# Gate and up of a SwiGLU feed-forward as 2x2 block products, seven in place of eight for three of eight k-tile pairs

## The chip, the core and the metric

One core of a Trainium2 chip runs the whole kernel. The metric is the device time of one execution in microseconds (us); smaller is better. The kernel before was timed three times: 2159.31, 2161.99 and 2163.21 us, with a median of 2161.99 us.

The engines are named as in the profile: PE is the matrix engine (PEld its weight loads, which run beside the products), DVE the vector engine, ACT the scalar engine, POOL the general one, SP the queue that issues the DMAs.

## What is computed

Two decoder layers over a sequence of 256 tokens of width 2048, float32. Layer 0 has a mixer with stick-breaking and differential attention heads, layer 1 a latent-attention mixer; each mixer, and each feed-forward, is followed by a layer norm of the residual sum. The change concerns the feed-forward, of which there is one in each layer:

```python
FFN_DIM = -(-8 * D_MODEL // (3 * 256)) * 256      # 5632

def swiglu_ffn(x, w_gate, w_up, w_down):
    return (jax.nn.silu(x @ w_gate) * (x @ w_up)) @ w_down

for layer in range(DEPTH):                        # 2
    ...
    x = layer_norm(DN_ALPHA * x + mix, ln_g[layer, 0], ln_b[layer, 0])
    x = layer_norm(DN_ALPHA * x + swiglu_ffn(x, ffn_w_gate[layer], ffn_w_up[layer], ffn_w_down[layer]),
                   ln_g[layer, 1], ln_b[layer, 1])
```

## The kernel before

**Precision.** Every large product is made of three. Each float32 operand is split into a rounded part hi (type fp32r) and the rest lo, and the product is hi·hi + hi·lo + lo·hi. `split` (L123) makes the parts: ACT copies the source into hi (L124), then DVE subtracts hi from the source and writes lo (L125). So each weight tile costs one ACT and one DVE instruction, and DVE's one waits for ACT's.

**Tiles.** The 256 tokens are two tiles t of 128 (NT = 2). The contraction over 2048 is 16 k-tiles of 128. The transposed x stands in SBUF for a whole feed-forward as hi and lo (`xTh`, `xTl`).

**A unit.** `ffn` (L448) walks through 11 chunks c of 512 hidden columns, in three parts of 4, 4 and 3 chunks. For one chunk (a unit) it calls `gemm` (L248) with gate and up side by side. For each of 16 k-tiles, `load` fetches 128x512 of gate and 128x512 of up into one 128x1024 tile w (two DMAs on SP, L273) and splits it. `products` (L278) then issues for each t six products of 128x128 by 128x512: hi·hi and hi·lo for gate, the same for up (L292, L293), then lo·hi for both (L295). A unit is 16 x 2 x 6 = 192 products into four PSUM banks. At its end `evac` (L461) does for each t a Silu of gate on ACT (L463) and a multiplication by up on DVE (L464). Two ticks later four PE transposes (L130) and a split (into `Rh`, `Rl`) turn the 128x512 result into the left side for the down product. After each part, two `gemm` calls (L494) multiply it by the weights of down and `add_to_x` (L402) adds into x; after the last one come the norm's statistics (L409) and the layer norm.

**What sets the order.** `tick` advances background work by one step after each k-tile. The source's order is only a priority: the program that puts the kernel together orders the instructions of each engine by when their inputs and buffers are there. `lag` (L275 on, used with `NORM_LAG` = 7 for the first unit of a feed-forward) lets t = 1 start seven k-tiles after t = 0, while the norm of the second tile ends; `advance` (L314, called at L328) says how far t = 1 may go.

**Buffers.** Weight tiles w have 5 buffers. The parts hi and lo have 6 buffers each; `halves` (L239) adds three more pairs out of buffers idle in this stage (`t6`, `gv`, `gk`) while `roomy` is set, which it is from the second half of the out projection to the end of the feed-forward: 9 pairs. In the mixers it is off: 6 pairs. PSUM has six banks "g" for products and two "m" for transposes and attention. The pool `ga` has two tiles of 128x2048, the norm's parameters among others; `stage` has four of 128x512.

Of the kernel before, what the change touches and what calls it, by code (L numbers as in the profile page):

```python
# [13 lines left out]
F32 = mybir.dt.float32  # L14
F32R = mybir.dt.float32r
I32 = mybir.dt.int32
AF = mybir.ActivationFunctionType
ALU = mybir.AluOpType
AX = mybir.AxisListType

P = 128
S = 256
NT = 2
D = 2048
KD = D // P
# [25 lines left out]
class Net:  # L51
# [11 lines left out]
    ATTENTION_DELAY = 3  # L63
    ACROSS = 3
    KEY_GROUP = 8
    HIDDEN_DELAY = 2
    BANKS = (6, 2)

# [170 lines left out]
    def halves(self, n):  # L239

        pools = [(self.hp, "h", self.lp, "l")] * self.BUFS[3]
        if self.roomy:
            pools += [(self.t6, "t6", self.gv, "v"), (self.gk, "kT", self.gv, "v"), (self.t6, "t6", self.t6, "t6")]
        hp, ht, lp, lt = pools[self.slot % len(pools)]
        self.slot += 1
        return hp.tile([P, n], F32R, tag=ht, name="h"), lp.tile([P, n], F32R, tag=lt, name="l")

    def gemm(self, src, kts, lhs, widths, evac=None, each=None, lag=0, apart=0, fine=0, across=0, before_end=None):  # L248
        nc = self.nc
        total = sum(widths)  # L250
        offs = [sum(widths[:c]) for c in range(len(widths))]
        ps, units = {}, {}

        def unit_width(k):
            return 512 if kts.index(k) < fine else 1024

        def load(k):
            units[k] = []
            aps = src(k)
            width = unit_width(k)  # L260
            for a0 in range(0, total, width):
                n = min(width, total - a0)
# [12 lines left out]
                self.split(hi, lo, w)  # L275
                units[k].append((hi, lo))

        def products(i, t, cs=None):  # L278
            k = kts[i]
            if i == 0:  # L280
                ps[t] = [self.psg.tile([P, 512], F32, tag="g", name="g") for _ in widths]
            first, last = i == 0, i == len(kts) - 1
            xh, xl = lhs(k, t)
            parts = []
            for c, n in enumerate(widths):
                width = unit_width(k)
# [12 lines left out]
            if last and evac:  # L299
                evac(t, ps[t])  # L300

        n = len(kts)
        tail = 2 if apart else 0
        second = 0

        def step(i, t):
            if i < n - max(tail, across):
                products(i, t)
            elif tail and i == n - 1:
                for c in range(len(widths)):  # L310
                    for k in range(n - tail, n):
                        products(k, t, slice(c, c + 1))

        def advance(end):  # L314
            nonlocal second
            while second < end:
                step(second, 1)
                second += 1

        for i in range(n):  # L320
            with ExitStack() as order:
                if fine:
                    for ins in self.first[:2 if i else 1]:
                        order.enter_context(self.tc.issue_after(ins.ins))
                load(kts[i])
            step(i, 0)
            self.tick()
            advance(min(i + 1 - lag, n - apart))  # L328
        if across:
            advance(n)  # L330
            for c in range(len(widths)):
                for t in range(NT):
                    for k in range(n - across, n):
                        products(k, t, slice(c, c + 1))
        advance(n - 1)
        if before_end:
            before_end()
        advance(n)
# [106 lines left out]
            self.norm_chunk(t)  # L445


    def ffn(self, layer, final):  # L448
        nc = self.nc
        wg, wu, wd = (self.io[n][layer] for n in ("ffn_w_gate", "ffn_w_up", "ffn_w_down"))  # L450
        parts = [range(0, 4), range(4, 8), range(8, 11)]
        for pi, part in enumerate(parts):
            self.new_res()
            for ci, c in enumerate(part):
                sl = slice(c * 512, (c + 1) * 512)

                def src(k):
                    rs = slice(k * P, (k + 1) * P)
                    return [((0, 512), wg[rs, sl]), ((512, 1024), wu[rs, sl])]

                def evac(t, ps, ci=ci):  # L461
                    sg = self.stage.tile([P, 512], F32, tag="st", name="sg")
                    nc.scalar.activation(sg, ps[0], AF.Silu)  # L463
                    nc.vector.tensor_tensor(sg, sg, ps[1], op=ALU.mult)  # L464

                    def transposed():
                        tp = self.bank()
                        self.transposes(tp, sg, 4)
                        ks = slice(4 * ci, 4 * ci + 4)
                        ts = slice(t * P, (t + 1) * P)  # L470
                        self.split(self.Rh[:, ks, ts], self.Rl[:, ks, ts], tp.rearrange("p (k n) -> p k n", k=4))

                    self.later(self.HIDDEN_DELAY, transposed)

                self.gemm(src, range(KD), self.from_x, [512, 512], evac, lag=self.NORM_LAG if c == 0 else 0)
                self.roomy = True
            n = 4 * len(part)
            last = pi == len(parts) - 1
            self.stats = {}
            k0 = part[0] * 4  # L480
            for half in range(2):
                if last and half == 1:
                    self.norm_params(layer, 1)

                def src(k, half=half, k0=k0):
                    return [((0, 1024), wd[(k0 + k) * P:(k0 + k + 1) * P, half * 1024:(half + 1) * 1024])]

                def each(t, c, ps, half=half, pi=pi, last=last):
                    self.add_to_x(t, half * 2 + c, ps, pi == 0, last)
                    if last and half == 1 and c == 1:  # L490
                        self.layer_norm(t, final)

                before_next = last and half == 1
                self.gemm(src, range(n), self.from_res, [512, 512], each=each,  # L494
                          apart=self.TILES_APART if before_next else 0,
                          before_end=(lambda: self.turn(0, 0)) if before_next and not final else None)
        self.roomy = False
# [204 lines left out]
    def mixer1(self):  # L702
# [40 lines left out]
        def rope_key():  # L743
            ps = self.bank()
            for t in range(NT):
                o = ps[:, t * P:(t + 1) * P]
                for k in range(KD):
# [139 lines left out]
```

## Time and profile before

| | |
|---|---|
| median of three runs | 2161.99 us |
| the profiled execution, its own time | 2163.7 us |
| its span, first to last instruction | 2162.0 us |
| PE busy | 2137.5 us, 99% of the span |
| PE weight loads busy | 1765.7 us, 82% |
| DVE busy | 1191.2 us, 55% |
| ACT busy | 936.9 us, 43% |
| DMA | 399.56 MB, mean 185 GB/s |
| mean granted PE clock | 0.997 of full speed |

The profile is of one execution. An engine is busy while it runs an instruction; a share of busy time is a mean over stages. Products on PE overlap in the record, so the time that one takes is read from the distance between the starts of two, not from its own duration. The idle time of an engine is put down to whatever released it. In the view by stretch a row gives the stretch (us from the start of the span) and its length, then the busy us, with instruction counts, of PE, PEld, DVE, ACT and POOL, then the granted PE clock, the DMA share and GB/s. In a timeline a row gives start, duration, engine, line, operation, out<-in and, in brackets, the idle time before it and what ended it; several alike in a row are merged (x2, x4).

### The profile page before, as it was taken

The page shows a single profiled execution, that of the slowest core. Times are in us where ns is not written, and L with a number is a line of the kernel's source. Part 1 is how long each engine was busy: PE and PEld are TensorE (multiplying, and loading weights), DVE is VectorE, ACT ScalarE, POOL GpSimd, SP SyncE. Part 2 cuts the span into 40 slices and gives each one's busy share as a digit, 9 for nine tenths or more (in the row PEclk, how much of TensorE's full clock was granted, in tenths as well). Part 3 has the DMA queues.
Part 4 walks back from the last instruction along what each step waited for, and adds up shares of the span by engine and source line. Part 5 has one row for each costly group of instructions (what it writes and reads, how often), then busy time and mean ns, then how long its engine had stood idle before and what let it go on. Part 6 is the DMA issues. An engine that isn't in the chain of part 4 may idle for free.

```text
span 2162.0 us, 25896 instructions
## 1 busy us (share of the span) xinstructions
PE 2137.5 (99%) x9734; PEld 1765.7 (82%) x9734; DVE 1191.2 (55%) x1340; ACT 936.9 (43%) x1111; POOL 51.9 (2%) x71
## 2 busy tenths in 40 slices
PE   8999999999999999999999999999999999999997
PEld 7888888888888888888887788888888888888886
DVE  7545566754554455444546665675544554445545
ACT  4554445354433444434424456444444344434441
POOL 0001010000000000000000100000000000000000
PEclk9999999999999999999999999999999999999999
DMA  7654647465556655566645443746556665556662
GB/s 261 196 164 147 194 142 249 146 221 188 193 187 195 190 189 187 193 197 190 222 151 156 160 138 103 257 142 224 186 191 193 192 192 185 191 193 192 191 228 77
DMA packets 171949, 399.56 MB, mean 185 GB/s; under 512 B 20400, under 2 KB 21040, under 8 KB 170800
## 3 DMA queue, kind: packets, MB, share of 16 engines
q1 hardware_dynamic: 171824, 397.91, 57.2%
q8 instruction: 76, 1.25, 0.2%
q14 instruction: 49, 0.40, 0.1%
HBM read 395.74 MB, written 2.10 MB: 184 GB/s over the span
## 4 chain that ended last, share of the span: by engine, by line
PE 93%; DVE 3%; issue 2%; ACT 1%; DMA 1%; POOL 0%; SPq 0%; DVEq 0%; POOLq 0%; ACTq 0%
PE g L293 29%; PE g L292 29%; PE g L295 29%; PE m L130 2%; DVE l L125 1%; PE m L560 0%; PE m L840 0%; PE m L841 0%; DVE x L438 0%; DMA x<-x 0%; DVE x L437 0%; DMA w<-sb_diff_w_out 0%; ACT sc L581 0%; ACT h L124 0%; DVE bs L409 0%
## 5 line engine op out<-in xcount | busy, mean ns | idle before, releaser
L125 DVE TENSOR_TENSOR l<-w,h 128x1024 fp32r<-128x1024 f32 (+1 forms) x737 | 892.2, 1219 | 836.9 <-ACT h L124 793.8
L124 ACT ACTIVATE h<-w 128x1024 fp32r<-128x1024 f32 (+1 forms) x737 | 769.5, 1053 | 1023.0 <-PE g L295 783.6
L292 PE MATMUL g<-h,xTh 128*128 128x512 f32 x1856 | 732.6, 396 | 1.0 <-ACT xTh L124 0.7
L293 PE MATMUL g<-l,xTh 128*128 128x512 f32 x1856 | 724.5, 392 | 0.5 <-DVE l L125 0.5
L295 PE MATMUL g<-h,xTl 128*128 128x512 f32 x1856 | 575.4, 391 | 0.0
L295 PEld LDWEIGHTS g<-h,xTl 128*128 128x128 f32 x1856 | 349.6, 188 | 73.8
L292 PEld LDWEIGHTS g<-h,xTh 128*128 128x128 f32 x1856 | 349.5, 189 | 73.3 <-ACT h L124 2.4
L293 PEld LDWEIGHTS g<-l,xTh 128*128 128x128 f32 x1856 | 349.8, 189 | 71.8 <-DVE l L125 1.8
L292 PE MATMUL g<-h,Rh 128*128 128x512 f32 x960 | 377.9, 394 | 0.0
L293 PE MATMUL g<-l,Rh 128*128 128x512 f32 x960 | 374.9, 390 | 0.0
L295 PE MATMUL g<-h,Rl 128*128 128x512 f32 x960 | 299.0, 390 | 0.0
L295 PEld LDWEIGHTS g<-h,Rl 128*128 128x128 f32 x960 | 180.3, 188 | 37.8
L292 PEld LDWEIGHTS g<-h,Rh 128*128 128x128 f32 x960 | 180.4, 188 | 36.7 <-DVE v L816 0.3
L293 PEld LDWEIGHTS g<-l,Rh 128*128 128x128 f32 x960 | 180.6, 188 | 36.2
L405 DVE SCALAR_TENSOR_TENSOR x<-x,g 128x512 f32<-128x512 f32 x64 | 40.9, 681 | 37.8 <-PE g L295 37.7
L124 ACT ACTIVATE Rh<-m 128x512 fp32r<-128x512 f32 x60 | 35.8, 596 | 58.3 <-PE m L130 41.5
L138 POOL TENSOR_TENSOR rr<-rv,mhalf 128x1 f32<-128x1 f32 (+1 forms) x16 | 13.0, 815 | 1703.2 <-DVE rv L136 1703.2
L125 DVE TENSOR_TENSOR Rl<-m,Rh 128x512 fp32r<-128x512 f32 x60 | 41.5, 691 | 20.1 <-ACT Rh L124 16.4
L463 ACT ACTIVATE sg<-g 128x512 f32<-128x512 f32 x44 | 26.2, 596 | 19.5 <-PE g L295 18.4
L464 DVE TENSOR_TENSOR sg<-sg,g 128x512 f32<-128x512 f32 x44 | 29.8, 684 | 7.6 <-ACT sg L463 7.6
L124 ACT ACTIVATE xTh<-m 128x512 fp32r<-128x512 f32 x30 | 17.7, 591 | 29.8 <-PE m L130 29.8
L130 PE MATMUL m<-ident,x 128*128 128x128 f32 x128 | 22.1, 288 | 8.2 <-DMA x<-x 6.0
(172 smaller groups left out, 853.5 us busy)
## 6 DMA issues: line engine op xcount, KB each, us to landing
w<-ffn_w_gate SPq DMA_DIRECT2D x352, 256.0 KB, 2.7
w<-ffn_w_up SPq DMA_DIRECT2D x352, 256.0 KB, 3.0
w<-ffn_w_down SPq DMA_DIRECT2D x176, 512.0 KB, 3.7
w<-sb_diff_w_in SPq DMA_DIRECT2D x95, 512.0 KB, 4.3
w<-sb_diff_w_out SPq DMA_DIRECT2D x32, 512.0 KB, 4.7
w<-mla_w_out SPq DMA_DIRECT2D x32, 512.0 KB, 4.3
w<-mla_w_in SPq DMA_DIRECT2D x16, 512.0 KB, 3.6
w<-mla_w_kv_up SPq DMA_DIRECT2D x16, 512.0 KB, 4.5
```

Of the source, the lines that this page charges most:

```text
L124: a = self.nc.vector.tensor_copy(hi, src) if whole else self.nc.scalar.activation(hi, src, AF.Copy)
L125: b = self.nc.vector.tensor_tensor(lo, src, hi.bitcast(F32), op=ALU.subtract)
L130: self.nc.tensor.transpose(ps[:, k * P:(k + 1) * P], src[:, k * P:(k + 1) * P], self.ident)
L138: nc.gpsimd.tensor_tensor(r, v, self.mhalf[:, 0:shape[1]], op=ALU.pow)
L292: nc.tensor.matmul(o, xh, hi, start=first, stop=False)
L293: nc.tensor.matmul(o, xh, lo, start=False, stop=False)
L295: nc.tensor.matmul(o, xl, hi, start=False, stop=last)
L405: nc.vector.scalar_tensor_tensor(xs, xs, ALPHA if first else 1.0, ps, op0=ALU.mult, op1=ALU.add)
L463: nc.scalar.activation(sg, ps[0], AF.Silu)
L464: nc.vector.tensor_tensor(sg, sg, ps[1], op=ALU.mult)
```

## The change

The first unit of each feed-forward (c = 0) stays as it was. The other ten are made by `joint_unit`. There the two token tiles and the two k-tiles of a pair j form a 2x2 matrix A of 128x128 blocks, gate and up of these k-tiles a 2x2 matrix B of 128x512 blocks, and the results are C11 (t = 0, gate), C12 (t = 0, up), C21 and C22. For the pairs 2, 4 and 6 the eight block products become seven (each still of three): the left sides are sums of x blocks, named S1 to S4, and the right sides are sums of weight blocks. They accumulate in seven PSUM banks p1 to p7 instead of four. The other five pairs have eight block products into p2 to p5, arranged so that they fit these accumulators, one of them with the left side D = x(t=0) − x(t=1).

`joint_forms` makes D for five pairs and S1 to S4 for three, once in a feed-forward, as background steps of the first unit that reach into the second: seven subtractions or additions on DVE, 22 PE transposes in seven groups, and seven splits. The forms lie in the buffers that `roomy` lent, so `roomy` is switched off from the eighth k-tile of the first unit on, and is on again for the last down product alone. `advance` is changed as well: once t = 1 has begun it takes up two k-tiles at each step until it has caught up.

```diff
+    JOINT_PAIRS = (2, 4, 6)
...
-            advance(min(i + 1 - lag, n - apart))
+            advance(min(i + 1 - lag if i < lag else second + 2, i + 1, n - apart))
+            if i + 1 == lag + 1 and lag:
+                self.roomy = False
...
+    def joint_forms(self):
+        nc = self.nc
+        for _ in range(12):
+            yield
...
+        difference(0, 2, 1)
+        yield
+        s1 = paired("S1", a21, a22, ALU.add)
+        yield
+        s2 = paired("S2", s1, a11, ALU.subtract)
+        yield
+        paired("S4", a12, s2, ALU.subtract)
+        yield
+        paired("S3", a11, a21, ALU.subtract)
+        yield
+        difference(3, 7, 2)
+        yield
+        difference(7, 8, 1)
+
+    def joint_unit(self, wg, wu, sl, hidden):
...
+        def add(name, a, b, first=False, last=False):
+            if name not in ps:
+                ps[name] = (self.bank() if name == "p7" else
+                            self.psg.tile([P, 512], F32, tag="g", name="g"))
+            o = ps[name]
+            nc.tensor.matmul(o, a[0], b[0], start=first, stop=False)
+            nc.tensor.matmul(o, a[0], b[1], start=False, stop=False)
+            nc.tensor.matmul(o, a[1], b[0], start=False, stop=last)
...
+        def plain(j):
+            b = []
+            for k in (2 * j, 2 * j + 1):
+                rs = slice(k * P, (k + 1) * P)
+                w = load(lambda w: [(w[:, 0:512], wg[rs, sl]), (w[:, 512:1024], wu[rs, sl])])
+                b.append(halves([None, w]))
+            ops = []
+            for k, (g, u) in zip((2 * j, 2 * j + 1), b):
+                a1, a2 = self.from_x(k, 0), self.from_x(k, 1)
+                ops.append((("p2", a1, g), ("p5", a2, u), ("p3", self.form["D", k], u), ("p4", a2, g)))
+            return ops
...
+        def joint(j):
+            two = lambda w: w.rearrange("p (k n) -> p k n", k=2)
+            wa = load(lambda w: [(two(w), pair(wg, j))])
+            wb = load(lambda w: [(two(w), pair(wu, j))])
+            b11, b21, b12, b22 = wa[:, 0:512], wa[:, 512:1024], wb[:, 0:512], wb[:, 512:1024]
+            t = self.ga.tile([P, 4, 512], F32, tag="A", name="T")
+            a = halves([None, wa])
+            v.tensor_tensor(t[:, 0], b12, b11, op=ALU.subtract)
+            v.tensor_tensor(t[:, 1], b22, t[:, 0], op=ALU.subtract)
+            b = halves([b22])
+            c = halves([None, t[:, 0:2].rearrange("p k n -> p (k n)")])
+            v.tensor_tensor(t[:, 2], b22, b12, op=ALU.subtract)
+            v.tensor_tensor(t[:, 3], b21, t[:, 1], op=ALU.subtract)
+            d = halves([None, t[:, 2:4].rearrange("p k n -> p (k n)")])
+            f = lambda n: self.form[n, j]
+            k1, k2 = 2 * j, 2 * j + 1
+            return (("p1", self.from_x(k1, 0), a[0]), ("p2", self.from_x(k2, 0), a[1]), ("p3", f("S4"), b[0]),
+                    ("p5", f("S1"), c[0]), ("p6", f("S2"), c[1]), ("p7", f("S3"), d[0]), ("p4", self.from_x(k2, 1), d[1]))
...
+        c1, u2, u3, c22 = tile("c1"), tile("u2"), tile("u3"), tile("c22")
+        nc.scalar.activation(c1, ps["p1"], AF.Copy)
+        v.tensor_tensor(u2, c1, ps["p6"], op=ALU.add)
+        v.tensor_tensor(u3, u2, ps["p7"], op=ALU.add)
+        ops = plain(n - 1)
+        for i in range(4):
+            for k in range(2):
+                add(*ops[k][i], last=k == 1)
+            if i == 0:
+                v.tensor_tensor(c1, c1, ps["p2"], op=ALU.add)
+                nc.scalar.activation(c1, c1, AF.Silu)
+            elif i == 1:
+                v.tensor_tensor(u2, u2, ps["p5"], op=ALU.add)
+                v.tensor_tensor(c22, u3, ps["p5"], op=ALU.add)
+            elif i == 2:
+                v.tensor_tensor(u2, u2, ps["p3"], op=ALU.add)
+                v.tensor_tensor(c1, c1, u2, op=ALU.mult)
+                hidden(0, c1)
+            else:
+                v.tensor_tensor(u3, u3, ps["p4"], op=ALU.add)
+                nc.scalar.activation(u3, u3, AF.Silu)
+                v.tensor_tensor(u3, u3, c22, op=ALU.mult)
+                hidden(1, u3)
...
+                if c:
+                    self.joint_unit(wg, wu, sl, hidden)
+                    continue
...
-                self.gemm(src, range(KD), self.from_x, [512, 512], evac, lag=self.NORM_LAG if c == 0 else 0)
-                self.roomy = True
+                self.background(self.joint_forms())
+                self.gemm(src, range(KD), self.from_x, [512, 512], evac, lag=self.NORM_LAG)
...
+                self.roomy = before_next
```

## Rows read from the trace of the kernel before

**Rows 1.** The page: the span, and busy time by engine with instruction counts.

```profile
span 2162.0 us, 25896 instructions
...
PE 2137.5 (99%) x9734; PEld 1765.7 (82%) x9734; DVE 1191.2 (55%) x1340; ACT 936.9 (43%) x1111; POOL 51.9 (2%) x71
```

**Rows 2.** The page: the chain that ended last, shares by engine and by line.

```profile
PE 93%; DVE 3%; issue 2%; ACT 1%; DMA 1%; POOL 0%; SPq 0%; DVEq 0%; POOLq 0%; ACTq 0%
PE g L293 29%; PE g L292 29%; PE g L295 29%; PE m L130 2%; DVE l L125 1%; PE m L560 0%; PE m L840 0%; PE m L841 0%; DVE x L438 0%; DMA x<-x 0%; DVE x L437 0%; DMA w<-sb_diff_w_out 0%; ACT sc L581 0%; ACT h L124 0%; DVE bs L409 0%
```

**Rows 3.** Busy time by stretch: mixer (6 buffer pairs), unit 7, a first unit.

```profile
220.00:266.00 46.00, 46.00 (x204) 38.12 (x203) 22.46 (x20) 20.10 (x21) 0.00 (x0) 1.00 0.69 206
...
806.20:850.70 44.50, 44.50 (x202) 36.87 (x201) 22.56 (x21) 19.05 (x21) 0.00 (x0) 1.00 0.59 194
...
407.50:453.60 46.10, 45.65 (x213) 36.98 (x211) 33.45 (x39) 22.52 (x26) 0.99 (x1) 1.00 0.63 201
```

**Rows 4.** Timeline of PE inside unit 7: start, duration, what.

```profile
808.69 0.39 PE L292 MATMUL g<-h,xTh 128*128 128x512 f32 x1
...
810.05 0.39 PE L292 MATMUL g<-h,xTh 128*128 128x512 f32 x1
...
811.42 0.60 PE L130 MATMUL m<-ident,sg 128*128 128x128 f32 x4
811.77 0.48 PE L292 MATMUL g<-h,xTh 128*128 128x512 f32 x1
```

**Rows 5.** Groups by line and form: count, busy us, mean ns, idle before.

```profile
L125 DVE TENSOR_TENSOR l<-w,h 128x1024 fp32r<-128x1024 f32 x727 | 885.7, 1227 | 835.6 <-ACT h L124 792.6 <-DMA w<-ffn_w_gate 39.7 <-DMA w<-ffn_w_up 2.3
L124 ACT ACTIVATE h<-w 128x1024 fp32r<-128x1024 f32 x727 | 763.6, 1059 | 1017.3 <-PE g L295 781.1 <-PE g L293 199.8 <-DMA w<-ffn_w_up 8.1
...
L464 DVE TENSOR_TENSOR sg<-sg,g 128x512 f32<-128x512 f32 x44 | 29.8, 684 | 7.6 <-ACT sg L463 7.6
...
L125 DVE TENSOR_TENSOR l<-w,h 128x512 fp32r<-128x512 f32 x10 | 6.8, 684 | 1.2 <-ACT h L124 1.2
```

**Rows 6.** Timeline of DVE near the end, instructions back to back.

```profile
2118.01 1.28 DVE L405 SCALAR_TENSOR_TENSOR x<-x,g 128x512 f32<-128x512 f32 x2
...
2122.78 4.65 DVE L125 TENSOR_TENSOR l<-w,h 128x1024 fp32r<-128x1024 f32 x4
2141.61 0.69 DVE L405 SCALAR_TENSOR_TENSOR x<-x,g 128x512 f32<-128x512 f32 x1 [14.19 <-PE g L295]
2142.33 0.69 DVE L409 BATCH_NORM_STATS2 bs<-x 128x6 f32<-128x512 f32 x1
```

**Rows 7.** Timeline of DVE through unit 7, the last of its part.

```profile
805.90 1.23 DVE L125 TENSOR_TENSOR l<-w,h 128x1024 fp32r<-128x1024 f32 x1 [1.49 <-ACT h L124]
807.05 0.68 DVE L464 TENSOR_TENSOR sg<-sg,g 128x512 f32<-128x512 f32 x1
...
817.75 1.23 DVE L125 TENSOR_TENSOR l<-w,h 128x1024 fp32r<-128x1024 f32 x1 [0.27 <-ACT h L124]
...
831.35 1.23 DVE L125 TENSOR_TENSOR l<-w,h 128x1024 fp32r<-128x1024 f32 x1 [1.50 <-ACT h L124]
...
849.94 1.23 DVE L125 TENSOR_TENSOR l<-w,h 128x1024 fp32r<-128x1024 f32 x1 [2.59 <-ACT h L124]
851.08 0.68 DVE L464 TENSOR_TENSOR sg<-sg,g 128x512 f32<-128x512 f32 x1
```

**Rows 8.** Timeline of SP in the same unit: the DMA issues.

```profile
816.91 0.33 SPq L273 DMA_DIRECT2D w<-ffn_w_gate  x1
...
819.00 38.41 SPq L273 DMA_DIRECT2D w<-ffn_w_down  x15
```

**Rows 9.** Timeline of ACT in the same unit: a hi part.

```profile
830.26 1.06 ACT L124 ACTIVATE h<-w 128x1024 fp32r<-128x1024 f32 x1 [1.66 <-PE g L295]
```

**Rows 10.** Waits over the whole span: who for whom, us, times, longest.

```profile
DVE l L125 <- ACT h L124: 793.8, 525, 5.5
ACT h L124 <- PE g L295: 783.6, 515, 16.6
```

More of the change, by code (lines that the diff above doesn't have):

```diff
@@ L445, in turn, with turned, joined, difference @@
             self.norm_chunk(t)
+    def joint_forms(self):
+        nc = self.nc
+        for _ in range(12):
+            yield
+        x = [a.rearrange("p (j k n) -> p j k n", j=KD // 2, k=2) for a in self.x]
+        J = self.JOINT_PAIRS
+        js = slice(J[0], J[-1] + 1, J[1] - J[0])
+        nj = len(J)
+        slots = [(self.gv, "v"), (self.gv, "v"), (self.gk, "kT"), (self.gk, "kT")] + [(self.t6, "t6")] * 3
+        self.form = {}
+        def turned(name, src, n):
+            pool, tag = slots.pop(0)
+            f = pool.tile([P, 2, 4, P], F32R, tag=tag, name=name)
+            tp = self.bank()
+            self.transposes(tp, src, n)
+            flat = lambda a: a.rearrange("p k n -> p (k n)")[:, 0:n * P]
+            self.split(flat(f[:, 0]), flat(f[:, 1]), tp[:, 0:n * P])
+            return f
+        def joined(name):
+            return self.stage.tile([P, 512], F32, tag="st", name=name)
+        def difference(j0, j1, step):
+            d = joined("d")
+            n = len(range(j0, j1, step))
+            v = d[:, 0:n * 256].rearrange("p (j m) -> p j m", j=n)
+            flat = lambda a: a[:, j0:j1:step].rearrange("p j k n -> p j (k n)")
+            nc.vector.tensor_tensor(v, flat(x[0]), flat(x[1]), op=ALU.subtract)
+            f = turned("D", d, 2 * n)
+            for i, j in enumerate(range(j0, j1, step)):
+                for k in range(2):
+                    self.form["D", 2 * j + k] = f[:, 0, 2 * i + k], f[:, 1, 2 * i + k]
+        def paired(name, a, b, op):
+            s = joined(name)
+            v = s[:, 0:nj * P].rearrange("p (j n) -> p j n", j=nj)
+            nc.vector.tensor_tensor(v, a, b, op=op)
+            f = turned(name, s, nj)
+            for i, j in enumerate(J):
+                self.form[name, j] = f[:, 0, i], f[:, 1, i]
+            return v
+        a11, a12, a21, a22 = (x[t][:, js, k, :] for t in range(2) for k in range(2))
+        difference(0, 2, 1)
[11 more added lines that the diff above has]
+        difference(7, 8, 1)
@@ new lines, in joint_unit, with load, halves, pair @@
+    def joint_unit(self, wg, wu, sl, hidden):
+        nc = self.nc
+        v = nc.vector
+        ps = {}
+        def add(name, a, b, first=False, last=False):
[6 more added lines that the diff above has]
+            nc.tensor.matmul(o, a[1], b[0], start=False, stop=last)
+        def load(parts):
+            w = self.wp.tile([P, 1024], F32, tag="w", name="w")
+            for dst, ap in parts(w):
+                self.load_ins = nc.sync.dma_start(out=dst, in_=ap)
+            return w
+        def halves(srcs):
+            hi, lo = self.halves(512 * len(srcs))
+            if len(srcs) == 2 and srcs[0] is None:
+                self.split(hi, lo, srcs[1])
+            else:
+                for i, a in enumerate(srcs):
+                    cs = slice(i * 512, (i + 1) * 512)
+                    self.split(hi[:, cs], lo[:, cs], a)
+            return [(hi[:, i * 512:(i + 1) * 512], lo[:, i * 512:(i + 1) * 512]) for i in range(len(srcs))]
+        def plain(j):
[9 more added lines that the diff above has]
+            return ops
+        def pair(w, j):
+            return w[2 * j * P:(2 * j + 2) * P, sl].rearrange("(k p) n -> p k n", p=P)
+        def joint(j):
[16 more added lines that the diff above has]
+                    ("p5", f("S1"), c[0]), ("p6", f("S2"), c[1]), ("p7", f("S3"), d[0]), ("p4", self.from_x(k2, 1), d[1]))
+        J = self.JOINT_PAIRS
+        n = KD // 2
+        made = {}
+        for j in range(n - 1):
+            if j in J:
+                for name, a, b in joint(j):
+                    add(name, a, b, first=j == J[0] and name in ("p1", "p6", "p7"), last=j == J[-1] and name in ("p1", "p6", "p7"))
+                self.tick()
+                self.tick()
+            else:
+                for ops in plain(j):
+                    for name, a, b in ops:
+                        add(name, a, b, first=name not in made)
+                        made[name] = True
+                    self.tick()
+        tile = lambda name: self.stage.tile([P, 512], F32, tag="st", name=name)
+        c1, u2, u3, c22 = tile("c1"), tile("u2"), tile("u3"), tile("c22")
[4 more added lines that the diff above has]
+        for i in range(4):
+            for k in range(2):
+                add(*ops[k][i], last=k == 1)
[9 more added lines that the diff above has]
+                hidden(0, c1)
+            else:
+                v.tensor_tensor(u3, u3, ps["p4"], op=ALU.add)
+                nc.scalar.activation(u3, u3, AF.Silu)
+                v.tensor_tensor(u3, u3, c22, op=ALU.mult)
+                hidden(1, u3)
+            if i % 2:
+                self.tick()
@@ L455, in ffn, with transposed, hidden @@
                 sl = slice(c * 512, (c + 1) * 512)
+                def transposed(t, sg, ci=ci):
+                    tp = self.bank()
+                    self.transposes(tp, sg, 4)
+                    ks = slice(4 * ci, 4 * ci + 4)
+                    ts = slice(t * P, (t + 1) * P)
+                    self.split(self.Rh[:, ks, ts], self.Rl[:, ks, ts], tp.rearrange("p (k n) -> p k n", k=4))
+                def hidden(t, sg, transposed=transposed):
+                    self.later(self.HIDDEN_DELAY, lambda: transposed(t, sg))
+                if c:
+                    self.joint_unit(wg, wu, sl, hidden)
+                    continue
                 def src(k):
@@ L459, in src, with evac @@
                     return [((0, 512), wg[rs, sl]), ((512, 1024), wu[rs, sl])]
-                def evac(t, ps, ci=ci):
+                def evac(t, ps):
                     sg = self.stage.tile([P, 512], F32, tag="st", name="sg")
@@ L464, in evac @@
                     nc.vector.tensor_tensor(sg, sg, ps[1], op=ALU.mult)
[L466 to L473, printed above, removed]
-                self.gemm(src, range(KD), self.from_x, [512, 512], evac, lag=self.NORM_LAG if c == 0 else 0)
-                self.roomy = True
+                    hidden(t, sg)
+                self.background(self.joint_forms())
+                self.gemm(src, range(KD), self.from_x, [512, 512], evac, lag=self.NORM_LAG)
             n = 4 * len(part)
```

## The prediction

> **What bounds the kernel now.** I read the page first. PE is busy 2137.5 of 2162.0 us, and DVE 1191.2 [rows 1]; the chain that ended last is 93% PE, three lines of products making up 87% of it [rows 2]. So fewer products on PE mean less time, as long as nothing else takes their place. The view by stretch narrows it to the place of the change: a unit of gate and up lasts 44.50 us, PE is busy in all of it at a granted clock of 1.00 (the level of 2.4 GHz), DVE in 22.56, ACT in 19.05 [rows 3]. The timeline of PE gives the price of a product: six of them from 808.69 to 810.05, 1.36 / 6 = 0.2267 us each [rows 4]. 192 of them are 43.5 us; the 0.97 us that are left of 44.50 are the unit's two groups of four transposes, so 0.49 a group, 0.12 a transpose.
>
> DVE and ACT idle because they are far ahead: lo waits for hi (793.8 us in all), and hi waits until PE frees a buffer (783.6 us) [rows 10]. A turn is short: hi 830.26 to 831.32 [rows 9], lo 831.35 to 832.58 [rows 7], 2.3 us. And the order on DVE is not that of the source. The last gate DMA of unit 7 was issued at 816.91, and behind it come those of down [rows 8]; from 817.75 to 849.94 DVE made 13 lo parts, of which at most the five tiles that w can hold were still gate and up. So at least eight were down's, though the unit's multiplication at 851.08 stands ahead of them in the source [rows 7]. Work that must wait is passed by work that need not. This matters most below.
>
> **Products removed.** Three pairs per unit lose one block product of three each: 9 x 20 units x 0.2267 = 40.8 us off PE, which is the bound in these units.
>
> **Transposes added.** 22 per layer in seven groups, 44 x 0.12 = 5.3 us onto PE. PE has almost no idle time to put them in: 0.45 us in a first unit [rows 3]. Their DVE part is seven sums and seven splits of at most 512 columns, 14 x 0.69 = 9.7 us per layer at most; DVE is idle for 12.6 of 46.1 us in the first unit [rows 3], and three of the seven steps run in the second. I take nothing; if that cover were gone it would be 0 to 9.7 us per layer.
>
> **DVE in a joint unit.** A lo part of 1024 columns lasts 1.23 us, an instruction of 512 columns 0.68 to 0.69, from PSUM or SBUF [rows 5]. Back to back they come closer: four of 1024 in 4.65, so (4.65 - 1.23) / 3 = 1.14 apart, and 512 ones 0.60 apart; one that needs the result just before it comes 0.72 later (2141.61 to 2142.33) [rows 6]. A joint unit has 19 of 1024 (ten in the plain pairs, three in each joint pair) and 26 of 512: three lo parts, twelve weight sums, nine at the unit's end, two of the hidden result. Back to back that is 19 x 1.14 + 26 x 0.60 = 37.3 us, end to end 19 x 1.23 + 26 x 0.69 = 41.3. PE needs 183 x 0.2267 + 0.97 = 42.45. DVE goes from half to nearly nine tenths of the unit but stays below PE. I take 37.3, since rows 6 are of just such streams. ACT gets 19 hi parts and eight of 512 columns, at most 27 x 1.06 = 28.6 us: no bound.
>
> The Trainium skill ("VectorE: DVE Perf Modes", section "The DRAIN you can't avoid") says that the next operation does not start until the pipe is empty. By that rule DVE would need the 41.3 us and leave PE a cover of 1.1 us per unit; the trace differs, with starts 0.09 us before the last end [rows 6].
>
> **The waits that the change adds.** A joint pair is a chain between two engines: sums 0 and 1, hi, lo, sums 2 and 3, hi, lo. In the source's order DVE would stand from 0 a lo part, 1.14 and 1.86 the sums, 2.46 a small lo; hi of the sums ends at 3.61, lo at 3.64; 4.78 and 5.38 the sums, hi ends at 7.13, lo at 7.16, free at 8.30. That is 6.44 of work and 1.86 of waiting. Behind it on DVE wait the lo parts of later tiles, and PE behind those. What covers it are the six buffer pairs. A joint pair takes four and a plain one two, so a ring is 21 + 24 = 45 products, 10.2 us. A plain tile's buffer is needed again 10.2 - 2.7 = 7.5 us after it is free, and its turn is 2.3, so DVE may be 5.2 us behind before PE waits. At the start of a unit there are two more plain tiles: the first joint pair's parts are due 12 to 15 us after the unit begins, and I count them done some 5 us earlier, with the work of the old unit's end taken in. So I take no wait of PE from this; in full it is 3 x 1.86 = 5.6 us of DVE per unit, 42.9 with the work.
>
> **The accumulators.** The seven use every bank "g" and one "m". The least cover is at p4: its last product of a unit ends about 0.16 us after 42.45 (0.39 us against a distance of 0.23 [rows 4]), DVE must add it (0.69), and the next unit writes p4 after nine products, 2.04 us. So DVE may be 1.2 us late, one long instruction. I take 0.25 us of PE waiting per unit for this and all other seams, 5 us in all; the ends are 0 and 1.7 (below).
>
> **Buffers, DMA and the order of t = 1.** Nine pairs become six for most of the feed-forward. The mixer has six, and PE is busy 46.00 of 46.00 us there with DMA at 206 GB/s [rows 3]; a joint unit asks for 194 x 44.50 / 42.45 = 203. A joint pair holds both w tiles until its last sum, and SP's later issues stand behind; SP was 34 us ahead [rows 7, 8], three tiles fewer leave 26. It issues six DMAs fewer per unit. The new `advance` moves the same products. k-tile 9 of a first unit finds its buffer freed 24 products, 5.4 us, before it is due; a turn takes 2.3. I take nothing; bounds -0.45 (the idle time there now) to +1 us per layer.
>
> **The sum.** The profiled execution took 2163.7 us, 1.7 around its span, and lies 1.7 above the median of the runs shown. 2163.7 - 40.8 + 5.3 + 5.0 = 2133.2; against the median 2131.5, say 2131. Without any wait it is 2126.5.
>
> **Rivals.** (1) The forecast: PE stays the bound, waits under 0.6 us a unit, 2125 to 2139. Chance 0.62. For it: 5 us of DVE's time free in each unit, and an order that passes waiting work.
>
> (2) Part is given back: DVE is behind by more than its cover at some seam of each unit, at p4 or in the joint pairs, and PE waits about 1 us: 2126.5 + 20 = 2147, up to 2160 at 1.7. For it: nearly nine tenths busy with six buffers instead of nine, and sums that wait for DMA, hi and PE by turns. Chance 0.20.
>
> (3) Slower: DVE becomes the bound by waiting inside the joint pairs. If its order there is the source's, a unit takes it 42.9 us, and about 3.2 more behind PE at the unit's end (the accumulators come 1.36 apart, then a Silu): 46.1, 1.6 above the 44.50 of now. 2163.7 - 1.7 + 5.3 + 32 = 2199. It begins to cost at 42.45 - 37.3 = 5.2 us of waiting per unit and decides the sign at (40.8 - 5.3) / 20 = 1.8 above that, 7.0. For it: waits of 1.86 per joint pair are in the source; against it rows 7 and 8. Chance 0.13.
>
> (4) No change: DVE's instructions do not overlap. 41.3 and the same 3.2 us at the end are 44.5, the unit of before, so the change doesn't shorten PE's time but fills it with waits: 2162 to 2167, counted here as the same. Against it: rows 6. Chance 0.05. [...]
>
> **How the numbers follow.** About 0.2%, 4 us, is what can be told from no change. Faster by more: (1) and (2), 0.82. Same: 0.05. Slower: 0.13. The range runs from 2122 (no wait, the idle time of the first units gained, and the runs' spread of 2 to 3 us) to 2160, the end of (2); it leaves out (3) and (4).
>
> **What would show it.** In the new profile PE should have 9734 - 180 + 44 = 9598 products and transposes, a joint unit should last 42.5 to 43.0 us with PE busy throughout, and DVE be busy in about 37 to 41 of them. ACT's hi should still wait mostly for PE, not PE for DVE. Wrong it would be if PE's lines showed idle time ended by DVE (lo parts, or the additions of p4) in every unit, or a unit lasted over 44.3 us.

## The result, and the profile after

The changed kernel takes 2121.99 us (median of four runs, 2121.04 to 2122.52) against 2160.9 of the kernel before on the same chip; the ratio is 0.982, with a 95% interval of 0.980 to 0.984. It is faster, by the mechanism of the forecast (PE the bound, fewer products), and the time lies 9 us below the point of 2131 and 0.01 us below the lower end of the range. So two things are to be found: what became of the 5 us of waiting that were counted, and where some 6 us come from that were not.

The page of the changed kernel (span, busy time by engine, and the chain that ended last by engine and by line), to be held against [rows 1, 2]:

```profile
span 2120.3 us, 26192 instructions
...
PE 2097.8 (99%) x9598; PEld 1734.3 (82%) x9598; DVE 1521.1 (72%) x1868; ACT 1047.1 (49%) x1265; POOL 52.1 (2%) x71
...
PE 94%; DVE 2%; issue 2%; DMA 1%; ACT 1%; POOL 0%; SPq 0%; DVEq 0%; POOLq 0%; ACTq 0%
PE g L293 17%; PE g L294 16%; PE g L296 16%; PE g L528 12%; PE g L526 12%; PE g L527 12%; PE m L131 3%; PE m L527 1%; PE m L528 1%; PE m L526 1%; DVE l L126 0%; PE m L742 0%; PE m L1022 0%; PE m L1023 0%; DMA w<-sb_diff_w_in 0%
```

PE has the 9598 products and transposes that were counted. DVE works 330 us more, and its share of the chain is 2%, not more than before. One joint unit, by stretch, against the 44.50 us of [rows 3] (same columns):

```profile
760.81:803.18 42.37, 42.37 (x192) 35.18 (x191) 37.91 (x47) 24.08 (x27) 0.00 (x0) 1.00 0.63 199
```

PE is busy in all of it, DVE in 37.91 (37.3 was the estimate). The other joint units are alike: within a part, from the last Silu of one (L616) to that of the next, it is 42.37 to 42.41 us in all 14 places of both layers. The same unit on DVE's timeline:

```profile
768.70 2.96 DVE L126 TENSOR_TENSOR l<-w,h 128x1024 fp32r<-128x1024 f32 x3
771.58 0.69 DVE L573 TENSOR_TENSOR T<-w,T 128x512 f32<-128x512 f32 x1
772.18 2.52 DVE L126 TENSOR_TENSOR l<-T,h 128x1024 fp32r<-128x1024 f32 x2
776.13 0.69 DVE L568 TENSOR_TENSOR T<-w 128x512 f32<-128x512 f32 x1 [1.43 <-DMA w<-ffn_w_up]
...
786.15 1.22 DVE L126 TENSOR_TENSOR l<-w,h 128x1024 fp32r<-128x1024 f32 x1 [1.12 <-ACT h L125]
788.83 1.23 DVE L126 TENSOR_TENSOR l<-w,h 128x1024 fp32r<-128x1024 f32 x1 [1.45 <-ACT h L125]
```

Before a joint pair's last sum (L573) three other lo parts are fitted in, and behind it come two lo parts of sums (l<-T) almost without a gap: the waits of 1.86 us that the source's order holds per pair are not there. DVE does wait, for weights still under way and for hi parts. Those wait in turn for buffers that PE has yet to free, as in [rows 10], which means that DVE is ahead. The waits over the whole span:

```profile
ACT h L125 <- PE g L296: 487.6, 317, 12.5
DVE l L126 <- ACT h L125: 437.6, 340, 5.5
ACT h L125 <- PE g L528: 226.6, 214, 2.1
```

The span can be cut at DVE's aggregations of the norms' statistics (L414 before, L417 after), which stand at the same places of both programs. Starts of the stretches in us before | after: 409.84 | 410.48, 1132.06 | 1114.03, 1142.78 | 1125.63, 1411.34 | 1387.71, 1422.92 | 1399.30, 2144.42 | 2102.45, end 2161.99 | 2120.35.

| stretch | before | after | difference |
|---|---|---|---|
| start and mixer of layer 0 | 409.84 | 410.48 | +0.64 |
| feed-forward of layer 0 | 722.22 | 703.55 | -18.67 |
| from the norm of t = 0 to that of t = 1 | 10.72 | 11.60 | +0.88 |
| latent mixer of layer 1 | 268.56 | 262.08 | -6.48 |
| norms of the mixer | 11.58 | 11.59 | +0.01 |
| feed-forward of layer 1 | 721.50 | 703.15 | -18.35 |
| end | 17.57 | 17.90 | +0.33 |

The feed-forwards give 37.0 us. The latent mixer gives 6.5, although the change is not meant for it. Its first 12 us before the change, by stretch, and PE's timeline at its start:

```profile
1143.00:1155.00 12.00, 9.11 (x30) 6.87 (x30) 11.86 (x18) 1.21 (x3) 0.92 (x1) 0.72 0.53 173
```

```profile
1144.42 0.38 PE L130 MATMUL m<-ident,x 128*128 128x128 f32 x2
1147.00 0.74 PE L130 MATMUL m<-ident,x 128*128 128x128 f32 x4 [2.21 <-DVE xTl L125]
1148.43 0.80 PE L292 MATMUL g<-h,xTh 128*128 128x512 f32 x1 [0.69 <-ACT xTh L124]
1149.02 0.63 PE L293 MATMUL g<-l,xTh 128*128 128x512 f32 x1
...
1153.29 1.05 PE L295 MATMUL g<-h,xTl 128*128 128x512 f32 x2
```

PE stood for 2.21 and 0.69 us, and the mean granted clock of these 12 us is 0.72: the twelve products whose starts lie from 1149.02 to 1153.72 come 0.427 us apart and not 0.227, at the lower of the clock's two levels (1.2 GHz). The same 12 us after the change have PE busy in 11.26 and the clock at 1.00 throughout:

```profile
1125.63:1137.63 12.00, 11.26 (x55) 8.82 (x54) 11.03 (x17) 3.74 (x5) 0.92 (x1) 1.00 0.29 101
```

### The profile page after: what moved, and what is told of

Its sections match the earlier page's. It is cut to its first block, busy times and chain, and to the rows that moved or that the text cites. A ratio compares the mean times of both kernels' runs of the same rounds, so it can differ in the third digit from the quotient of the medians.

```text
span 2120.3 us, 26192 instructions
## 1 busy us (share of the span) xinstructions
PE 2097.8 (99%) x9598; PEld 1734.3 (82%) x9598; DVE 1521.1 (72%) x1868; ACT 1047.1 (49%) x1265; POOL 52.1 (2%) x71
## 4 chain that ended last, share of the span: by engine, by line
PE 94%; DVE 2%; issue 2%; DMA 1%; ACT 1%; POOL 0%; SPq 0%; DVEq 0%; POOLq 0%; ACTq 0%
PE g L293 17%; PE g L294 16%; PE g L296 16%; PE g L528 12%; PE g L526 12%; PE g L527 12%; PE m L131 3%; PE m L527 1%; PE m L528 1%; PE m L526 1%; DVE l L126 0%; PE m L742 0%; PE m L1022 0%; PE m L1023 0%; DMA w<-sb_diff_w_in 0%
## 5 line engine op out<-in xcount | busy, mean ns | idle before, releaser
L126 DVE TENSOR_TENSOR l<-w,h 128x1024 fp32r<-128x1024 f32 (+1 forms) x737 | 854.5, 1174 | 440.4 <-ACT h L125 435.9
L125 ACT ACTIVATE h<-w 128x1024 fp32r<-128x1024 f32 (+1 forms) x737 | 739.6, 1018 | 757.8 <-PE g L296 487.6
L526 PE MATMUL g<-h,xTh 128*128 128x512 f32 x780 | 305.5, 392 | 0.0
L528 PE MATMUL g<-h,xTl 128*128 128x512 f32 x780 | 304.1, 390 | 0.0
L527 PE MATMUL g<-l,xTh 128*128 128x512 f32 x780 | 304.1, 390 | 0.0
L293 PE MATMUL g<-h,xTh 128*128 128x512 f32 x576 | 230.9, 405 | 1.2 <-ACT xTh L125 0.7
L294 PE MATMUL g<-l,xTh 128*128 128x512 f32 x576 | 225.1, 394 | 0.0
L296 PE MATMUL g<-h,xTl 128*128 128x512 f32 x576 | 179.9, 392 | 0.0
L125 ACT ACTIVATE h<-T 128x1024 fp32r<-128x1024 f32 x120 | 127.4, 1062 | 97.5 <-DVE T L569 41.9
L528 PEld LDWEIGHTS g<-h,xTl 128*128 128x128 f32 x780 | 146.5, 188 | 30.4
L527 PEld LDWEIGHTS g<-l,xTh 128*128 128x128 f32 x780 | 146.6, 188 | 29.7
L526 PEld LDWEIGHTS g<-h,xTh 128*128 128x128 f32 x780 | 146.5, 188 | 29.7
L126 DVE TENSOR_TENSOR l<-T,h 128x1024 fp32r<-128x1024 f32 x120 | 145.0, 1221 | 3.5 <-ACT h L125 1.7
L293 PEld LDWEIGHTS g<-h,xTh 128*128 128x128 f32 x576 | 108.5, 190 | 24.0 <-ACT xTh L125 2.0
L296 PEld LDWEIGHTS g<-h,xTl 128*128 128x128 f32 x576 | 108.2, 188 | 23.8 <-DVE xTl L126 0.8
L294 PEld LDWEIGHTS g<-l,xTh 128*128 128x128 f32 x576 | 108.6, 189 | 21.9 <-DVE l L126 1.1
```

The costliest lines, as they stand in the source:

```text
L125: a = self.nc.vector.tensor_copy(hi, src) if whole else self.nc.scalar.activation(hi, src, AF.Copy)
L126: b = self.nc.vector.tensor_tensor(lo, src, hi.bitcast(F32), op=ALU.subtract)
L526: nc.tensor.matmul(o, a[0], b[0], start=first, stop=False)
L527: nc.tensor.matmul(o, a[0], b[1], start=False, stop=False)
L528: nc.tensor.matmul(o, a[1], b[0], start=False, stop=last)
```

## Experiments: where the 6 us at the layer boundary come from

Two theories. **A, the phase of the buffers:** `halves` deals out the nine pairs in a circle. Ahead of the first feed-forward the kernel before has taken 129 pairs, in it 264; the twelve of the last down product are numbers 381 to 392, modulo nine 3 to 8 and then 0 to 5. The last six tiles, which t = 1 works on six k-tiles behind t = 0 (`TILES_APART`), hold the pairs 0 to 5: all the ordinary ones, and the only ones that the next mixer uses. In the changed kernel the feed-forward takes 324 (a joint pair takes four, not two), and the last six are 6, 7, 8, 0, 1, 2: three ordinary pairs are free. **B, the order of t = 1:** the new line in `advance` also works in the mixer's first product.

**The kernel before, phase moved.**

```diff
-                before_next = last and half == 1
+                before_next = last and half == 1; self.slot += 6 * before_next
```

> The kernel before, with the counter of buffer pairs moved on by six ahead of the last down product of a feed-forward, so that of the six tiles that t = 1 still holds at its end three lie in the lent pairs and not all six in the ones that the next mixer uses. Theory A (the 6.5 us that the stretch from the norm's second aggregation to the out projection lost, 268.6 to 262.1 us, come from which pairs the last down product holds): that stretch falls to about 262 us, the PE stall of 2.2 us and the half clock behind it go, and the whole is 4 to 7 us shorter than the kernel before. Theory B (they come from the new order of t = 1 in advance): stretch 268.6, the whole within 2 us of before.

Measured: 2158.86 us (11 runs) against 2162.6 (21 runs), ratio 0.9983, interval 0.9974 to 0.9992. The first 12 us and the whole of the mixer, by stretch, and ACT's hi parts ahead of it:

```profile
1145.31:1157.31 12.00, 11.26 (x55) 8.79 (x54) 11.02 (x17) 3.74 (x5) 0.92 (x1) 1.00 0.29 98
1145.31:1407.87 262.56, 259.37 (x1293) 214.03 (x1292) 159.46 (x239) 132.24 (x233) 14.91 (x22) 1.00 0.49 160
```

```profile
1115.94 1.06 ACT L124 ACTIVATE h<-w 128x1024 fp32r<-128x1024 f32 x1 [1.65 <-PE g L295]
1118.66 1.06 ACT L124 ACTIVATE h<-w 128x1024 fp32r<-128x1024 f32 x1 [1.66 <-PE g L295]
1121.38 1.06 ACT L124 ACTIVATE h<-w 128x1024 fp32r<-128x1024 f32 x1 [1.66 <-PE g L295]
1124.10 1.06 ACT L124 ACTIVATE h<-w 128x1024 fp32r<-128x1024 f32 x1 [1.66 <-PE g L295]
1137.70 1.06 ACT L124 ACTIVATE h<-w 128x1024 fp32r<-128x1024 f32 x1 [12.54 <-PE g L295]
```

The same place in the kernel before, whose norm comes 1.65 us earlier:

```profile
1114.29 1.06 ACT L124 ACTIVATE h<-w 128x1024 fp32r<-128x1024 f32 x1 [1.66 <-PE g L295]
1131.96 1.06 ACT L124 ACTIVATE h<-w 128x1024 fp32r<-128x1024 f32 x1 [16.62 <-PE g L295]
```

With three pairs free, ACT and DVE make three more tiles (1118.66, 1121.38, 1124.10) before the down product ends; without them ACT waits 16.62 us. So when DVE turns to the norm of t = 1, t = 0 has products left to fill the time. The stretch falls by 6.0 us, as A says. The whole falls by 3.7 us, just below what A gave (4 to 7): in this profile 0.9 are lost again between the norms of t = 0 and t = 1, as in the changed kernel, and the start took 1.9 longer, in a stretch that this edit does not touch.

**The kernel before, with the new line of advance alone.**

```diff
-            advance(min(i + 1 - lag, n - apart))
+            advance(min(i + 1 - lag if i < lag else second + 2, i + 1, n - apart))
```

> The kernel before with the new line in advance alone (t = 1 takes two k-tiles a step). Theory A (buffer pairs): the stretch of the latent mixer stays near 268.6 us, stall and half clock stay, the whole within 2 us of before. Theory B (order of t = 1): the stretch falls to about 262 us, the whole 4 to 7 us shorter.

Measured: 2163.64 us, ratio 1.0005 (0.9996 to 1.0014).

```profile
1143.22:1155.22 12.00, 9.12 (x31) 6.83 (x30) 12.00 (x19) 1.42 (x3) 0.92 (x1) 0.72 0.51 164
1143.22:1411.31 268.09, 262.73 (x1297) 217.17 (x1296) 163.91 (x244) 132.19 (x233) 16.01 (x22) 0.99 0.50 161
```

Stall, low clock and stretch (268.09 against 268.56) stay: B falls.

**The changed kernel, phase moved back**, by `self.slot += 3 * before_next` in the same line, so that the last six tiles hold 0 to 5 again.

> The changed kernel, with the counter of buffer pairs moved on by three ahead of the last down product, so that t = 1 holds all six of the pairs that the next mixer uses, as in the kernel before. Theory A: the stall comes back, the stretch of the latent mixer rises from 262 to about 268 us and the whole to 2126 to 2129. Theory B: 262 us and 2122, as in the changed kernel.

Measured: 2126.56 us (2125.84 to 2127.91), ratio 0.9835 against before.

```profile
1125.21:1137.21 12.00, 9.11 (x43) 6.97 (x41) 12.00 (x20) 2.49 (x4) 0.92 (x1) 1.00 0.51 165
1125.21:1390.68 265.47, 260.06 (x1297) 214.96 (x1296) 163.67 (x244) 132.03 (x233) 14.90 (x22) 1.00 0.50 163
```

PE is busy in 9.11 of 12 us, as in the kernel before (its two gaps are 2.20 and 0.69 us), and the whole is longer than the changed kernel by 4.6 us, medians of separate series (3.5 by the two ratios to before). But in this trace the stretch rises by 3.4 us and not by 6, and the clock stays at 1.00. So by this one trace the 6 us fall in two: about 3 for the standing, and about 3 for the low clock behind it (12 products at 0.427 and not 0.227 us are 2.4 of them). The Trainium skill ("TensorE: Matmul & The Clock Gate", Part 1) says that the engine's clock is released by activity and falls back when it idles. Two of these traces show the fall right behind the stall, and this one shows the same stall without it, so a stall of this size may or may not bring it; what decides, no run here shows. The mean clock of whole executions varies in the same way, though it does not tell where the clock was low: of the 21 executions of the kernel before, 14 have 0.997 and 2163.1 us on the mean, seven have 0.998 or 0.999 and 2161.3. Of the five of this kernel three have 0.997, and they are not clearly longer (2125.84 to 2127.91, against 2126.33 for the profiled one at 0.999). The price of the low clock is thus 2 to 3 us in the kernel before, and known only roughly.

## Experiments: how much cover DVE has

Theory A here: an order that passes waiting work, and six buffer pairs, let DVE be filled nearly to PE's time. The rival is that the seams that the prediction named (p4, the chains in the joint pairs) have a microsecond or so, and that waiting starts there first.

**Additions beside the work.** `v.tensor_tensor(e, xs, xs, op=ALU.add)` of 384 columns, once or twice after each k-tile of the plain pairs in the loop. The last plain pair stands outside it, so there were 8 and 16 a unit instead of ten and twenty.

> The changed kernel with ten more DVE additions of 384 columns in each joint unit, results unused, about 0.46 us each (between the 0.33 of 256 and the 0.60 of 512 columns): DVE's work goes from 37.3 to about 41.9 us of the unit's 42.4. Theory A (six buffer pairs and an order that passes waiting work hide nearly all of DVE's free time): a unit of 42.4 to 43.0 us, 2122 to 2134 in all. Rival (the cover at p4 and in the joint chains is a microsecond or so and is used up first): 44 us or more a unit, over 2150.

> The same with twenty such additions a unit: DVE's work is 46.5 us, above PE's 42.4. Both theories say that DVE is the bound; A says that the unit is about DVE's work, 46.5 to 47.5 us and 2205 to 2225 in all; the rival adds waits of 3 us or more on top, a unit of over 49.5 and over 2265.

Measured: 2122.89 and 2122.58 us. Neither costs anything, but this tells nothing on the cover, because the additions didn't stay in the units. DVE's busy time by stretch in the kernel with two each, for these additions alone (columns: stretch, length, DVE busy with count, PE clock, DMA share, GB/s):

```profile
587.00:718.00 131.00, 31.91 (x64) 1.00 0.60 192
718.00:845.00 127.00, 0.00 (x0) 1.00 0.63 203
845.00:975.00 130.00, 23.79 (x48) 1.00 0.60 194
```

The second row covers three joint units, and none of their additions is in it; they have moved to stretches with down products, in the first and third rows, where DVE has time. Nothing needs their result, and what nobody waits for is put last. The expectation of 2205 to 2225 was wrong, since the load was not where it said.

**lo made twice.** A second, equal subtraction into lo for some plain tiles. PE's products wait for it, so it stays.

```diff
+                if k in (0, 2, 6, 10):
+                    v.tensor_tensor(self.last_lo, w, self.last_hi.bitcast(F32), op=ALU.subtract)
```

> The changed kernel, with the DVE subtraction that makes lo done twice over for four of the plain k-tiles (0, 2, 6, 10) of each joint unit, same result; PE's products wait for the second, so it can't move out of the unit. DVE's work: 37.3 + 4 x 1.14 = 41.9 us, PE's 42.4. Theory A (buffers and order hide nearly all of DVE's free time): a unit of 42.4 to 43.2, 2122 to 2138 in all. Rival (the waits inside the joint chains, 1.9 us a pair, can't be filled): 41.9 + 3 or more, 45 us a unit, 2170 and over.

> The same for eight of the ten plain k-tiles (0 to 3, 6, 7, 10, 11): DVE's work is 37.3 + 9.1 = 46.5 us, 4.1 above PE's. Theory A: the unit is DVE's work and about a microsecond, 46.5 to 48 us, 2200 to 2235 in all. Rival: 49.5 us or more, over 2260.

Measured: 2124.07 us (2122.91 to 2124.42) with four. The unit:

```profile
761.64:804.05 42.41, 42.41 (x193) 35.14 (x192) 42.38 (x50) 23.43 (x27) 0.00 (x0) 1.00 0.62 198
```

DVE is busy in 42.38 of 42.41 us, and PE in all of them. The other units within a part last 42.39 to 42.81 us, and the whole is 2.1 us longer than the changed kernel's, with overlapping intervals of the two ratios. The rival (45 us a unit) falls: in this unit no wait of the joint chains is left unfilled, and nearly all of DVE's free time is cover. With eight (tiles 0 to 3, 6, 7, 10, 11): 2177.17 us. The second and the third unit behind a down product, and what PE waited for over the span:

```profile
726.73:771.59 44.86, 42.74 (x187) 33.40 (x186) 44.41 (x52) 23.16 (x27) 0.00 (x0) 1.00 0.56 175
771.59:818.98 47.39, 44.90 (x193) 34.73 (x192) 46.88 (x54) 23.20 (x27) 0.00 (x0) 1.00 0.56 177
```

```profile
PEld g L527 <- DVE l L554: 45.1, 63, 1.4
PE g L527 <- DVE l L554: 23.2, 34, 1.0
```

Once DVE's work passes PE's, the unit is DVE's work: 47.39 us, with DVE busy in 46.88 (46.5 expected). The whole is 23 us below the expected 2200, because the units are not alike, as I had counted them. DVE gets ahead while down is multiplied: from the transposes of one part's last-but-one chunk to those of the next part's first it is 130.8 us here as in the changed kernel, so the first unit costs nothing more, and the second is only 2.5 us longer.

**Four joint pairs** (0, 2, 4, 6), with the forms made two ticks earlier.

> Seven products in four pairs (0, 2, 4, 6) instead of three, the forms made two ticks earlier. PE: 180 products, 41.7 us a unit; DVE 20 instructions of 1024 and 31 of 512 columns, 20 x 1.14 + 31 x 0.60 = 41.4 us. Theory A (DVE can be filled to within about 1 us of PE): a unit of 41.7 to 42.4 and 2108 to 2122. Rival (the joint pair at the unit's start collides with the end of the unit before, and chains cost DVE 1.9 us a pair): 43.5 us or more, over 2145.

Measured: 2145.04 us (2142.16 to 2146.38), at the lower edge of the rival's expectation (over 2145). A unit, and PE's waits over the span:

```profile
765.79:809.62 43.83, 42.45 (x189) 34.37 (x188) 42.01 (x52) 24.79 (x30) 0.00 (x0) 1.00 0.62 186
```

```profile
PE m L524 <- ACT h L125: 11.8, 8, 1.8
PE m L131 <- DVE Rl L126: 8.8, 6, 1.6
```

DVE's work is 42.01 us (41.4 by the sum), just above PE's 41.7, and the unit is 1.8 longer still. The units are not alike here: within a part they last 42.0 to 45.0 us. PE does wait at seams: p7 of the joint pair at the unit's start, for the hi part that ends the chain (L524), and the second group of transposes, which needs the "m" bank that p7 doesn't hold, for the split of the first (L131). In this unit the first is 1.2 of PE's 1.38 us of idle time. How much is DVE's work and how much the place of the pair isn't told apart. The phase of the buffers differs too (the last six tiles hold the pair 8 and the pairs 0 to 4), but it is not what costs: this profile is 22.2 us longer than the changed kernel's, and the two feed-forwards are 10.6 and 12.2 us longer.

**Four pairs, with sums on POOL.** `nc.gpsimd.tensor_tensor` for sums 0 and 2, or for 2 alone; the phase as in the changed kernel.

> Four joint pairs (0, 2, 4, 6), with two of the four weight sums of each pair (up minus gate of the first k-tile, up minus up) on POOL instead of DVE, and the counter of buffer pairs moved by seven so that the last down product holds the three lent pairs. DVE 20 x 1.14 + 23 x 0.60 = 36.6 us a unit, POOL 8 sums of about 1.29 us, 10.3 us; PE 180 products, 41.7. Theory A (four pairs failed by DVE's work alone): a unit of 41.7 to 42.1 and 2106 to 2116. Rival (the chain of a joint pair at the unit's start is what fails, and a slower sum or POOL and DVE hindering each other makes it longer): 42.9 us or more, over 2130.

> The same with one sum of each pair on POOL (up minus up). DVE 20 x 1.14 + 27 x 0.60 = 39.0 us a unit, PE 41.7. Theory A: 41.7 to 42.4 and 2106 to 2121. Rival: 42.9 or more, over 2130.

Measured: 2222.02 us (2216.14 to 2223.52) with two sums and 2164.82 with one, against 2145.04 with none. Both times lie in the rival's range, but the runs don't tell the two theories apart, since the sums moved to POOL made the instructions left on DVE longer. Groups by line of the kernel with two (POOL's sums, then the DVE sum that waits for one of them), and of the one with one (POOL's sums, DVE's sums, and a lo part of the same size for comparison):

```profile
L570 POOL TENSOR_TENSOR T<-w 128x512 f32<-128x512 f32 x80 | 127.4, 1592 | 0.0
L566 POOL TENSOR_TENSOR T<-w 128x512 f32<-128x512 f32 x80 | 113.1, 1414 | 1106.9 <-DMA w<-ffn_w_up 1018.7 <-DVE u L607 40.0 <-DVE l L126 27.1
...
L567 DVE TENSOR_TENSOR T<-w,T 128x512 f32<-128x512 f32 x80 | 110.7, 1384 | 142.6 <-POOL T L566 142.6
```

```profile
L570 POOL TENSOR_TENSOR T<-w 128x512 f32<-128x512 f32 x80 | 135.3, 1691 | 1154.0 <-DMA w<-ffn_w_up 1144.7 <-DVE l L126 9.3
...
L567 DVE TENSOR_TENSOR T<-w,T 128x512 f32<-128x512 f32 x80 | 82.2, 1028 | 1.5
L566 DVE TENSOR_TENSOR T<-w 128x512 f32<-128x512 f32 x80 | 72.1, 901 | 75.2 <-DMA w<-ffn_w_up 75.2
L126 DVE TENSOR_TENSOR l<-w,h 128x512 fp32r<-128x512 f32 x90 | 61.4, 682 | 4.8 <-ACT h L125 4.8
```

A sum takes POOL 1.41 to 1.69 us on the mean, and the DVE sums of L566 and L567 grow on the mean from 0.69 us to 0.90, 1.03 and 1.38, while the last sum (L571) and the small lo parts keep 0.68 to 0.69. These means mix two cases, as two DVE sums of the kernel with two on POOL show, the first with POOL idle, the second beside a sum of POOL (DVE's timeline, then POOL's):

```profile
752.49 0.68 DVE L567 TENSOR_TENSOR T<-w,T 128x512 f32<-128x512 f32 x1
759.13 1.78 DVE L567 TENSOR_TENSOR T<-w,T 128x512 f32<-128x512 f32 x1 [1.19 <-POOL T L566]
```

```profile
759.05 1.31 POOL L570 TENSOR_TENSOR T<-w 128x512 f32<-128x512 f32 x1
```

Of the 80 sums of this line, 54 run beside one of POOL's and take 1.72 us on the mean; the other 26 take 0.68. The Trainium skill ("SBUF — State Buffer", section "Who interferes with whom") says that a DVE instruction with two SBUF inputs contends with a GpSimd one that reads SBUF, and that the order of issue decides which of the two is blocked. The trace agrees: a DVE sum that runs beside POOL's takes 1.72 us and not 0.68. With two sums, DVE also waits 142.6 us for POOL's. What was taken off DVE comes back as blocking and as a longer chain. A third part is the clock: in these units it is at its lower level in 14 short stretches, each of which begins within 2 us of the end of a wait of PE of 1.8 to 3.2 us. Two of them lie in this stretch (granted clock 0.93):

```profile
1750.00:1800.00 50.00, 44.59 (x187) 36.06 (x186) 41.82 (x44) 24.76 (x30) 11.98 (x8) 0.93 0.52 167
```

Its mean over the span is 0.987 with two sums, against 0.998 with none. That is some 48 us more at the lower level, worth at most 22 of the 77 us (an estimate: 48 x 0.200 / 0.427, as if PE had had a product ready all the time).

## Why the prediction was right and where it failed

The prediction's terms against the profiles (spans 2162.0 and 2120.3 us, difference 41.7):

- **Products removed, 40.8 us.** 20 x (44.50 - 42.37) = 42.6. Right. 183 x 0.2267 = 41.49 leave 0.88 us of the unit for its two groups of transposes, which now come one behind the other, where 0.97 had been counted: 20 x 0.09 = 1.8.
- **Transposes added, 5.3 us.** The feed-forwards lost 37.0, so what was added to them is 42.6 - 37.0 = 5.6. The size is right, as far as a remainder can show it.
- **DVE in a joint unit, 37.3 us.** 37.91 measured. The 41.3 of the end-to-end sum, and rival 4 with them, are refuted by it, and by the four double lo parts: they made DVE 4.5 us busier for 2 us in all. The prediction gives only half of what the Trainium skill's section "The DRAIN you can't avoid" says: it goes on that a next operation which isn't held back starts earlier. The starts 0.09 us before the last end [rows 6] agree with that.
- **The waits, 5 us.** This step failed. "I take 0.25 us of PE waiting per unit for this and all other seams" should have been nothing. The p4 seam and the chains don't show in any joint unit (42.37 to 42.41 us in all 14 places), and DVE could take up its last free time before PE waited. The same reading of [rows 7, 8] that set rival 3 aside, that the order passes what must wait, says this too; I used it against rival 3 and not for my own term. Rivals 2 and 3 fall with it.
- **Buffers and the order of t = 1, 0 taken, -0.45 to +1 us per layer.** This bound failed. It was read from the idle time of a first unit of a feed-forward, while the change also altered how many pairs a feed-forward takes from the circle of nine, and with that which of them are held at the border of the layers. The mixer's stretch fell by 6.5 us, of which 0.9 came back between the norms. The two moves of the phase show the cause and, with the clock, roughly the size; the new `advance`, which the prediction named in this place, has no effect in the kernel before (ratio 1.0005). The stall was in the trace of before: 2.21 and 0.69 us of idle time of PE at 1147.00 and 1148.43, and a clock of 0.72 over 12 us.
- **The rest** is +1.0 us at the start and the end. -37.0 - 6.5 + 0.9 + 1.0 = -41.6.

Without the 5 us of waiting and with the boundary's 5.6 the prediction's own sum gives 2131.5 - 5.0 - 5.6 = 2120.9, 1 us below the measured median. That the time lies so near the lower end of the range is luck: the range reached down to it by the spread of the runs and the idle time of the first units, not by the border of the layers. The medians differ by less than the profiles (38.9 us over the four runs of before, 40.6 over the later 21), because the profiled run of before, at 2163.7, was a long one.

## What to carry to other kernels

A bound by one engine can be traded for work on another until the other's sum, taken back to back, reaches the first one's, if the order of the instructions lets work that can run pass work that must wait: here DVE could be filled to 42.38 of 42.41 us for 2 us in all, and another 4.5 us of work in each unit (46.88) made the whole 55 us longer than the changed kernel. Before an edit is costed at nothing, see what else counts on what it changes: a circle of buffers that is dealt out more often ends at another place, and what stands idle at a border far from the edit can move by microseconds. An extra load that is to measure cover must be one that something waits for, or it moves to where there is room.

## What the runs showed of the hardware that was not expected

- After the same stall of PE (9.1 of 12 us busy) the clock was granted at 0.72 on the mean in two traces and at 1.00 in a third; the fall was worth some 2 to 3 us.
- Beside a POOL subtraction of 512 columns, DVE's own instructions of 512 columns with two SBUF inputs took up to 1.78 us and not 0.69. With one or two of each pair's four sums on POOL, which had been idle there, the kernel of four pairs was 20 and 77 us slower; part of the 77 is the lower clock behind PE's waits.
